# Pool's long element-wise operations in pieces, first norm's squares added on VectorE, second layer's first norm summed earlier, three Newton steps in place of four

## The chip, the cores and the metric

One core of one Trainium2 chip runs the whole program. The metric is the device time of one execution in microseconds (us). The time before is 2428.57 us, the median of 3 runs (2425.60 to 2429.08).

## The reference

A trunk of two layers on 16 learned meta tokens followed by 512 tokens, so T = 528, with rows of 1024 channels. Each layer is a norm, one input projection, two parallel branches, a gated merge, and an MLP. All weights and data are float32.

```
xn = rms_norm(h, norm1_g)                       # h * rsqrt(mean(h*h) + EPS) * g
z, xbc, dt_raw, q, k, v, gates = split(xn @ w_in)
y_ssd  = ssd_mixer(z, xbc, dt_raw, ...)         # conv, silu, chunked scan, 8 groups, group norm
y_attn = sliding_window_attention(q, k, v, ...) # rms_norm and rotary on q and k, window 128, sinks
merged = g_ssd * (y_ssd @ w_ssd_down) + g_attn * (y_attn @ w_attn_down)
h = h + merged @ w_o
h = h + square(relu(rms_norm(h, norm2_g) @ w_mlp_up)) @ w_mlp_down
```

The norms of q and k are over 64 channels of a head. The output is h without the meta tokens.

## The kernel before

Activations lie transposed: 128 channels on the partitions, tokens along the columns, so h is 8 rows of 128x528 (`h(k)`). Every dense product is made in a split of float32 into two rounded parts, `hi` and `lo = x - hi`: each weight tile (1024x128, `wraw`) is loaded by DMA, rounded by ScalarE into `whi`, and VectorE or GpSimd (Pool) subtracts to get `wlo`; TensorE then runs three passes of 8 matmuls (hi by hi, lo by hi, hi by lo) for each span of columns (266 or 264, or 512 in the parts that leave the meta tokens out). There are 172 weight tiles a layer, and two buffers each for `wraw`, `whi` and `wlo`.

The order on every engine is written by a planner in Python, the class `Flow`. It keeps a clock for each engine (`F.t`), costs each instruction by a formula, and pins the program order. Dense products run in a fixed order; the rest are generator tasks in queues (`w` for weights, `post`, `misc`, `tail`, `chunk`, `attn`), which `tick` steps forward between matmuls once the plan has their inputs ready. So a change of one cost moves instructions of all engines further on. `tt_any` (line 434 ff.) gives an element-wise operation to Pool (`G`) if the plan has it end there earlier than on VectorE (`V`) with a margin; the `wlo` subtractions, the rotary products and parts of attention and of the y rows go through it.

The places that the change touches:

- **Program start.** DMAs on SP's queue load `h` (8 rows), then the first constants (`cst`, whose `ones` column every sum needs), then the weights of v. For each row ScalarE squares it (`sq`), and TensorE adds over channels with five matmuls by `ones`, one for each chunk of tokens, into five banks; `rms_tok` turns the sums into the norm's factor `rt` (five small operations on VectorE, one power on Pool). `bcast_tok` spreads it over partitions (TensorE), VectorE multiplies `h` by it, ScalarE writes `hnh`, VectorE `hnl`, and the products with the weights of v (`wvh`, `wvl`, 288 columns: v and dt) begin.
- **Layer 1, first norm.** The products of v start from rows of h without the norm's factor (`hgh`, `hgl`; 8 rows, hi and lo in turn), since the factor of a token is applied afterwards. `norm` adds squares over channels, as `cst,acc` and `cst,sq` matmuls; a task that `tick` steps when its rows are planned to be ready. The normed rows (`hnh`, `hnl`) are made from its factor by `normal_row` and are needed by the first tile of k.
- **Norms of q and k.** `rsqrt` runs on VectorE: a start from integer arithmetic (`rqs`), then four Newton steps of three operations on 128x20 to 128x40 elements, then a copy. It is called once for k and twice for q in each layer, and the attention scores of the heads wait for it.
- **Pool's operations.** `wlo` is one operation of 128x1024, `q` (lo part of the queries) 64x512, the rotary product `qa`, `kn` 128x528 or 128x512, `t` the same, and in `tail` one of the two products by the gate 128x528 or 128x512.

Of the kernel before, what the change touches and what calls it, by code (L numbers as in the profile page):

```python
# [17 lines left out]
P = 128  # L18
# [28 lines left out]
CCOL = {}  # L47
# [307 lines left out]
def hybrid_trunk_kernel(ctx: ExitStack, tc: tile.TileContext, h0, params, consts, rope, wdt, w, out,  # L355
# [80 lines left out]
    def tt_any(out, a, b, op, spare=None):  # L436

        n = Engine.size(out)
        eng = G if max(F.t["g"], F.t["pe"]) + n * 2.09 + 125.0 < max(F.t["v"], F.t["pe"]) + n / 0.96 + (F.SPARE if spare is None else spare) else V
        eng.tensor_tensor(out=out, in0=a, in1=b, op=op)  # L440
# [151 lines left out]
    def rms_tok(sq, inv_n, cs, tag, rows=(), bank="ps", sums=None):  # L592


        if not sums:
            yield {bank: 1, "after": rows, "data": lambda: [x[:, CHUNKS[cs[0]][0]:sum(CHUNKS[cs[-1]])] for x in sq()]}
            ps = Slot("ps")
            for c in cs:
                t0 = CHUNKS[c][0]
                x = sq()  # L600
                for i in range(len(x)):
                    mm(ps.t[:, c:c + 1], x[i][:, t0:t0 + P], C("ones"), start=i == 0, stop=i == len(x) - 1)
# [3 lines left out]
        for c in cs if sums else (cs[0],):  # L606
            y, z = (x[:, c:c + 1], sums[c].t[:, 0:1]) if sums else (x, ps.t[:, c:cs[-1] + 1])
            V.tensor_scalar(out=y, in0=z, scalar1=inv_n, scalar2=EPS, op0=ALU.mult, op1=ALU.add)
        for z in sums or (ps,):
            z.free()  # L610
# [61 lines left out]
    F.dma(par[:, 0, 0:KD], params[:, 0, 0:KD])  # L672
    for k in range(KD):
        F.dma(h(k), h0[:, k, :])
    few = CCOL["low"][0]
    F.dma(cst[:, 0:few], consts[:, 0:few])
# [12 lines left out]
    sums = [Slot("ps") for _ in CHUNKS]  # L689
    for k in range(KD):  # L690
        sq = Slot(min(("zs", "sq", "xh", "raw"), key=lambda n: F.rings[n].at()), "sq")
        S.activation(out=sq.t, in_=h(k), func=AF.Square)
        for c in range(5):
            t0 = CHUNKS[c][0]
            mm(sums[c].t[:, 0:1], sq.t[:, t0:t0 + P], C("ones"), start=k == 0, stop=k == KD - 1)
        F.end = F.t["pe"]
        sq.free()
# [16 lines left out]
    for l in range(depth):  # L714
# [144 lines left out]
        for k in range(KD + 1):  # L859
            F.force(rows_[k:k + 1])  # L860
            if k < KD:
# [43 lines left out]
        def rope_tile(kind, spans, m, dst, c_lo):  # L905
# [15 lines left out]
            def rest():  # L921
# [8 lines left out]
                G.tensor_tensor(out=dst[:, lo:T], in0=qx[:, lo:T], in1=cosg[:, lo:T], op=ALU.mult)  # L930
# [19 lines left out]
        def rsqrt(x, t):  # L950
# [5 lines left out]
            for _ in range(4):  # L956
# [324 lines left out]
        def tail(gr, zs, cs):  # L1281
# [6 lines left out]
            for j in range(2):  # L1288
                (G if j else V).tensor_tensor(out=xs[j], in0=xs[j], in1=sq[j][:, a:b], op=ALU.mult)
# [456 lines left out]
```

## Time and profile before

| | |
|---|---|
| time, median of 3 runs | 2428.57 us |
| time of the profiled execution | 2423.47 us |
| span of the profiled execution | 2421.3 us |
| TensorE busy | 2361.0 us (98%) |
| VectorE (DVE) busy | 1313.1 us (54%) |
| ScalarE (ACT) busy | 1024.9 us (42%) |
| Pool busy | 1101.8 us (46%) |
| mean granted clock of TensorE | 0.995 |

A busy VectorE is counted from the start of an instruction to its end, with what it waits inside the instruction. Busy TensorE says nothing of its clock. Most instructions of VectorE, ScalarE and Pool are issued by one helper and stand under line L348, matmuls under L431 and transposes under L434, so they are told apart by their tiles.

### The profile page before, as it was taken

The page shows a single profiled execution, that of the slowest core. Times are in us where ns is not written, and L with a number is a line of the kernel's source. Part 1 is how long each engine was busy: PE and PEld are TensorE (multiplying, and loading weights), DVE is VectorE, ACT ScalarE, POOL GpSimd, SP SyncE. Part 2 cuts the span into 40 slices and gives each one's busy share as a digit, 9 for nine tenths or more (in the row PEclk, how much of TensorE's full clock was granted, in tenths as well). Part 3 has the DMA queues.
Part 4 walks back from the last instruction along what each step waited for, and adds up shares of the span by engine and source line. Part 5 has one row for each costly group of instructions (what it writes and reads, how often), then busy time and mean ns, then how long its engine had stood idle before and what let it go on. Part 6 is the DMA issues. An engine that isn't in the chain of part 4 may idle for free.

```text
span 2421.3 us, 40518 instructions
## 1 busy us (share of the span) xinstructions
PE 2361.0 (98%) x16098; PEld 2148.4 (89%) x16098; DVE 1313.1 (54%) x2505; ACT 1024.9 (42%) x1999; POOL 1101.8 (46%) x659
## 2 busy tenths in 40 slices
PE   7999999999999999999999899999999999999999
PEld 7998999999999999999998778888987788888887
DVE  3686879787423444233247868787874145433221
ACT  3455665654422233223244456656554223333231
POOL 2734444465444334434435444445555544444443
PEclk9999999999999999999999999999999999999999
DMA  3323333343453322222232233334434433222222
GB/s 122 105 79 98 93 103 93 102 115 102 121 180 111 134 85 88 89 96 88 99 133 86 66 104 106 110 80 115 112 105 127 176 120 135 96 95 93 94 93 104
DMA packets 133578, 257.33 MB, mean 106 GB/s; under 512 B 16470, under 2 KB 66318, under 8 KB 133390
## 3 DMA queue, kind: packets, MB, share of 16 engines
q1 hardware_dynamic: 133390, 254.75, 33.1%
q8 instruction: 127, 2.08, 0.3%
q14 instruction: 61, 0.50, 0.1%
HBM read 232.03 MB, written 17.33 MB: 103 GB/s over the span
## 4 chain that ended last, share of the span: by engine, by line
PE 82%; DVE 12%; issue 2%; DMA 1%; ACT 1%; POOL 1%; SPq 0%; DVEq 0%; POOLq 0%; ACTq 0%
PE ps L431 80%; PE ps L434 2%; DVE at L348 2%; DVE raw L348 2%; DVE xb L348 1%; DVE rqs L348 1%; DVE xh L348 1%; DVE ar L348 1%; DMA gm<-ac_dram 1%; DVE gm L348 1%; DVE qa L348 0%; DVE hnl L348 0%; DVE es L348 0%; DVE h L348 0%; DVE mx L348 0%
## 5 line engine op out<-in xcount | busy, mean ns | idle before, releaser
L348 POOL TENSOR_TENSOR wlo<-wraw,whi 128x1024 fp32r<-128x1024 f32 x326 | 793.4, 2434 | 950.0 <-ACT whi L348 880.5
L348 ACT CAST whi<-wraw 128x1024 fp32r<-128x1024 f32 x340 | 355.4, 1045 | 708.0 <-PE ps L431 412.9
L431 PE MATMUL ps<-hnh,whi 128*128 128x266 f32 (+2 forms) x2048 | 398.7, 311 | 5.6 <-ACT hnh L348 4.8
L431 PE MATMUL ps<-hnl,whi 128*128 128x266 f32 (+2 forms) x2048 | 395.7, 310 | 0.0
L431 PE MATMUL ps<-hnh,wlo 128*128 128x266 f32 (+2 forms) x2048 | 389.6, 308 | 0.0
L431 PEld LDWEIGHTS ps<-hnh,whi 128*128 128x128 f32 x2048 | 304.4, 190 | 21.4 <-ACT hnh L348 6.2
L431 PEld LDWEIGHTS ps<-hnl,whi 128*128 128x128 f32 x2048 | 304.2, 190 | 15.1 <-issue 1.8
L431 PEld LDWEIGHTS ps<-hnh,wlo 128*128 128x128 f32 x2048 | 302.7, 190 | 15.3 <-issue 2.7
L348 DVE SCALAR_TENSOR_TENSOR h<-ps,h 128x264 f32<-128x264 f32 (+1 forms) x120 | 62.1, 518 | 308.6 <-PE ps L431 308.6
L348 DVE TENSOR_TENSOR hidl<-s,hidh 128x528 fp32r<-128x528 f32 (+1 forms) x64 | 116.8, 1824 | 87.9 <-ACT s L348 87.9
L431 PE MATMUL ps<-hgl,whi 128*128 128x264 f32 (+1 forms) x768 | 153.7, 322 | 1.3 <-DVE hgl L348 1.3
L431 PE MATMUL ps<-hgh,wlo 128*128 128x264 f32 (+1 forms) x768 | 153.3, 321 | 0.0
L431 PE MATMUL ps<-hgh,whi 128*128 128x264 f32 (+1 forms) x768 | 152.8, 320 | 0.0
L431 PE MATMUL ps<-hidl,whi 128*128 128x264 f32 (+1 forms) x768 | 152.7, 320 | 0.0
L431 PE MATMUL ps<-hidh,whi 128*128 128x264 f32 (+1 forms) x768 | 152.5, 320 | 0.0
L431 PE MATMUL ps<-hidh,wlo 128*128 128x264 f32 (+1 forms) x768 | 152.5, 320 | 0.0
L431 PE MATMUL ps<-y,whi 128*128 128x264 f32 (+1 forms) x768 | 137.0, 320 | 0.0
L431 PEld LDWEIGHTS ps<-hgl,whi 128*128 128x128 f32 x768 | 119.1, 189 | 12.4 <-DVE hgl L348 1.6
L431 PEld LDWEIGHTS ps<-hgh,wlo 128*128 128x128 f32 x768 | 119.3, 189 | 11.1
L431 PEld LDWEIGHTS ps<-hidl,whi 128*128 128x128 f32 x768 | 118.8, 188 | 11.0
L431 PEld LDWEIGHTS ps<-hidh,wlo 128*128 128x128 f32 x768 | 118.7, 188 | 11.1
L431 PEld LDWEIGHTS ps<-hidh,whi 128*128 128x128 f32 x768 | 118.6, 188 | 11.1
(220 smaller groups left out, 3949.5 us busy)
## 6 DMA issues: line engine op xcount, KB each, us to landing
wraw<-w_dram SPq DMA_DIRECT2D x344, 512.0 KB
gm<-ac_dram SPq DMA_DIRECT2D x64, 256.0 KB
et<-ac_dram SPq DMA_DIRECT2D x128, 64.0 KB
t<-au SPq DMA_DIRECT2D x48, 66.0 KB
h<-h_dram SPq DMA_DIRECT2D x8, 264.0 KB
at<-rope_dram SPq DMA_DIRECT2D x4, 528.0 KB
y_dram<-xb SPq DMA_DIRECT2D x4, 528.0 KB
yr<-y_dram SPq DMA_DIRECT2D x8, 264.0 KB
```

Of the source, the lines that this page charges most:

```text
L348: inst = fn(*a, **k)
L431: F.run("pe", cost, [o], [lhsT, rhs], PE.matmul(out=o, lhsT=lhsT, rhs=rhs, start=start, stop=stop))
L434: F.run("pe", 108.0 if in_.shape[1] > 64 else 60.0, [o], [in_], PE.transpose(out=o, in_=in_, identity=C("ident", k)[:, :k]))
```

## The change

1. `tt_any` issues an operation that goes to Pool and has 512 columns or more in pieces of at most 256 (for a tile of several rows: row by row where a row is longer). The rotary product on Pool is cut in two at column 264, the gate's product in `tail` in two halves.
2. At the start, the first constants are loaded after the fifth row of h and no longer after the eighth. The squares of the 8 rows are added on VectorE into the first (7 additions of 128x528), and TensorE sums that one row over channels with 5 matmuls into one bank, where it had 40 into five. While rows arrive, TensorE multiplies each of the first seven by itself (128x264, float32) into a bank that nothing reads.
3. In layer 1, before the products of row 5 for v, all rows of h are forced into the order and the norm's sums are issued.
4. `rsqrt` makes three Newton steps.

```
         eng = G if ... else V
-        eng.tensor_tensor(out=out, in0=a, in1=b, op=op)
+        if eng is V or n < 512:
+            eng.tensor_tensor(out=out, in0=a, in1=b, op=op)
+            return
+
+        if len(out.shape) == 2:
+            m = -(-n // 256)
+            at = [n * i // m for i in range(m + 1)]
+            for x, y in zip(at, at[1:]):
+                eng.tensor_tensor(out=out[:, x:y], in0=a[:, x:y], in1=b[:, x:y], op=op)
+            return
+        m = out.shape[1]
+        step = max(1, m * 256 // n)
+        for x in range(0, m, step):
+            y = min(x + step, m)
+            eng.tensor_tensor(out=out[:, x:y], in0=a[:, x:y], in1=b[:, x:y], op=op)
...
+    few = CCOL["low"][0]
     for k in range(KD):
         F.dma(h(k), h0[:, k, :])
-    few = CCOL["low"][0]
-    F.dma(cst[:, 0:few], consts[:, 0:few])
+        if k == 4:
+            F.dma(cst[:, 0:few], consts[:, 0:few])
...
-    sums = [Slot("ps") for _ in CHUNKS]
+    busy = Slot("ps")
+    kinds = ("zs", "sq", "xh", "raw")
+    total = None
     for k in range(KD):
-        sq = Slot(min(("zs", "sq", "xh", "raw"), key=lambda n: F.rings[n].at()), "sq")
+        sq = Slot(min(kinds, key=lambda n: F.rings[n].at()), "sq")
         S.activation(out=sq.t, in_=h(k), func=AF.Square)
-        for c in range(5):
-            t0 = CHUNKS[c][0]
-            mm(sums[c].t[:, 0:1], sq.t[:, t0:t0 + P], C("ones"), start=k == 0, stop=k == KD - 1)
-        F.end = F.t["pe"]
-        sq.free()
+        if k < KD - 1:
+            mm(busy.t[:, 0:T // 2], h(k)[:, 0:P], h(k)[:, 0:T // 2])
+        if total is None:
+            total = sq
+        else:
+            V.tensor_tensor(out=total.t, in0=total.t, in1=sq.t, op=ALU.add)
+            F.end = F.t["v"]
+            sq.free()
+    busy.free()
+    sums = Slot("ps")
+    for c in range(5):
+        t0 = CHUNKS[c][0]
+        mm(sums.t[:, c:c + 1], total.t[:, t0:t0 + P], C("ones"))
...
         for k in range(KD + 1):
             F.force(rows_[k:k + 1])
+            if l and k == KD - 3:
+
+                F.force(rows_)
+                while norm_t[0].needs.get("after") is not None:
+                    F.step(norm_t[0], F.queues["misc"])
...
-                G.tensor_tensor(out=dst[:, lo:T], in0=qx[:, lo:T], in1=cosg[:, lo:T], op=ALU.mult)
+                for x, y in ((lo, 264), (264, T)):
+                    G.tensor_tensor(out=dst[:, x:y], in0=qx[:, x:y], in1=cosg[:, x:y], op=ALU.mult)
...
-            for _ in range(4):
+            for _ in range(3):
...
-            for j in range(2):
-                (G if j else V).tensor_tensor(out=xs[j], in0=xs[j], in1=sq[j][:, a:b], op=ALU.mult)
+            V.tensor_tensor(out=xs[0], in0=xs[0], in1=sq[0][:, a:b], op=ALU.mult)
+            h_ = (b - a) // 2
+            for x, y in ((0, h_), (h_, b - a)):
+                G.tensor_tensor(out=xs[1][:, x:y], in0=xs[1][:, x:y], in1=sq[1][:, a + x:a + y], op=ALU.mult)
```

How the instructions move, at three places. A row is line, operation, output and inputs, size, and how often it stands in a row.

**TensorE at the program's start**, before:

```order
L431 MATMUL ps<-cst,sq 128x1 x40
L431 MATMUL ps<-cst,rt 128x16
L431 MATMUL ps<-cst,rt 128x128 x4
L431 MATMUL ps<-wvh,hnh_192 128x288 x10
L431 MATMUL ps<-wvl,hnh_192 128x288 x4
```

and after:

```order
L431 MATMUL ps<-h_80 128x264 x4
L431 MATMUL ps<-h_81 128x264 x3
L431 MATMUL ps<-cst,sq 128x1 x5
L431 MATMUL ps<-cst,rt 128x16
L431 MATMUL ps<-cst,rt 128x128 x4
L431 MATMUL ps<-wvh,hnh_164 128x288 x10
```

The 40 sums become 5, behind the seven products of h by itself; on VectorE the seven additions stand ahead of a single `rt<-ps 128x5`. VectorE also gets a subtraction `wvl<-wraw,wvh 128x7x128` and a `wvl<-rawdt,wvh 128x7x32` behind its first `hnl`, where it had 128x128 and 128x32; Pool has the smaller ones now.

**VectorE at layer 1's first norm**, from the factor `rt` to the first `dtx` (which waits for the last products of v), before:

```order
L348 TENSOR_SCALAR rt<-ps 128x5
L348 TENSOR_SCALAR na<-na 128x32
L348 TENSOR_TENSOR h_9718<-h_9718,ps 128x272
L348 TENSOR_TENSOR h_9718<-h_9718,ps 128x256
L348 SCALAR_TENSOR_TENSOR hnl_14216<-h_9718,par,hnh_14214 128x528
L348 SCALAR_TENSOR_TENSOR dtx<-ps,rt,par 128x32
```

and after (the products `h<-h,ps` of six rows of h stand there, of which these are the last two, where before there were four rows):

```order
L348 TENSOR_TENSOR h_10012<-h_10012,ps 128x272
L348 TENSOR_TENSOR h_10012<-h_10012,ps 128x256
L348 SCALAR_TENSOR_TENSOR hnl_14725<-h_10011,par,hnh_14723 128x528
L348 TENSOR_TENSOR h_10012<-h_10012,ps 128x272
L348 TENSOR_TENSOR h_10012<-h_10012,ps 128x256
L348 SCALAR_TENSOR_TENSOR hnl_14726<-h_10012,par,hnh_14724 128x528
L348 SCALAR_TENSOR_TENSOR dtx<-ps,rt,par 128x32
```

On TensorE the ten sums `cst,acc` and `cst,sq` stand behind 45 products of v, where they stood behind 68.

**Pool in layer 1 beside the norms of the first four tiles of q**, before:

```order
L348 TENSOR_TENSOR wlo<-wraw,whi 128x1024
L348 TENSOR_TENSOR q_14980<-qa_14591,q_14980 64x512
L348 TENSOR_TENSOR q_14986<-qa_14591,q_14986 64x512
L348 TENSOR_TENSOR qa_14592<-au,at 128x512
L348 TENSOR_TENSOR wlo<-wraw,whi 128x1024
L348 TENSOR_TENSOR qa_14592<-au,at 128x512
L348 TENSOR_TENSOR t_15015<-t_15015,at 128x512
```

and after:

```order
L348 TENSOR_TENSOR wlo<-wraw,whi 128x256 x4
L348 TENSOR_TENSOR q_15506<-qa_15102,q_15506 64x256 x2
L348 TENSOR_TENSOR q_15513<-qa_15102,q_15513 64x256 x2
L348 TENSOR_TENSOR qa_15103<-au,at 128x248
L348 TENSOR_TENSOR qa_15103<-au,at 128x264
L348 TENSOR_TENSOR wlo<-wraw,whi 128x256 x4
L348 TENSOR_TENSOR t_15479<-t_15479,at 128x256 x2
```

The same work in the same order, each operation cut in two or four. Over the whole program 326 operations `wlo` of 128x1024 on Pool become 1264 of 128x256 (316 weight tiles; VectorE makes 24 in place of 14).

## Rows read from the trace of the kernel before

**Rows 1.** The page's first part: busy us, share, instructions; and the clock by core.

```profile
PE 2361.0 (98%) x16098; PEld 2148.4 (89%) x16098; DVE 1313.1 (54%) x2505; ACT 1024.9 (42%) x1999; POOL 1101.8 (46%) x659
...
core 0: 2421.3 us, clock 0.995
```

**Rows 2.** Busy by stretch: us; PE, PEld, DVE, ACT, POOL; PEclk; DMA share, GB/s.

```profile
34.00:600.00 566.00, 552.87 (x4438) 523.25 (x4439) 441.37 (x1026) 321.43 (x775) 282.99 (x201) 1.00 0.34 98
600.00:1246.00 646.00, 643.15 (x5271) 639.80 (x5270) 230.69 (x328) 200.48 (x292) 270.01 (x130) 1.00 0.32 111
1246.00:1860.00 614.00, 588.31 (x3883) 513.36 (x3882) 470.60 (x982) 330.02 (x717) 300.06 (x216) 0.99 0.36 101
```

**Rows 3.** Waits of TensorE's matmuls from 34 us on: us in total, times, longest us.

```profile
PE ps L431 <- DVE ar L348: 13.3, 16, 2.2
...
PE ps L431 <- DVE rqk L348: 3.7, 1, 3.7
PE ps L431 <- POOL xdd L348: 2.2, 2, 1.7
```

**Rows 4.** Timeline of TensorE at the start: start us, us, work [idle before <-releaser].

```profile
11.39 17.20 PE L431 MATMUL ps<-cst,sq 128*128 128x1 f32 x80 [11.39 <-DMA cst<-consts_dram]
30.10 2.61 PE L431 MATMUL ps<-cst,rt 16*128 16x16 f32 x10 [1.51 <-POOL rt L348]
33.99 2.77 PE L431 MATMUL ps<-wvh,hnh 128*128 128x288 f32 x10 [1.28 <-ACT hnh L348]
```

**Rows 5.** Timeline of ACT at the start.

```profile
8.29 1.30 ACT L348 ACTIVATE sq<-h 128x528 f32<-128x528 f32 x2 [1.41 <-DMA h<-h_dram]
...
18.55 2.16 ACT L348 CAST wvh<-wraw 128x896 fp32r<-128x896 f32 x4
```

**Rows 6.** Timeline of DVE before layer 1: an addition like the new ones.

```profile
1232.28 0.70 DVE L348 TENSOR_TENSOR acc<-acc,sq 128x528 f32<-128x528 f32 x1
```

**Rows 7.** Timeline of PE and DVE at layer 1's first norm.

```profile
1254.63 0.28 PE L431 MATMUL ps<-cst,acc 128*128 128x1 f32 x2
...
1259.88 1.68 DVE L348 TENSOR_TENSOR h<-h,ps 128x272 f32<-128x272 f32 x4 [2.67 <-PE ps L431]
...
1260.52 5.46 PE L431 MATMUL ps<-wvl,hgh 128*128 128x288 f32 x40
...
1273.17 0.81 PE L431 MATMUL ps<-hnh,whi 128*128 128x264 f32 x2 [4.76 <-ACT hnh L348]
```

**Rows 8.** Timeline of Pool, DVE and PE at the norms of layer 1's first q tiles.

```profile
1335.70 2.34 POOL L348 TENSOR_TENSOR wlo<-wraw,whi 128x1024 fp32r<-128x1024 f32 x1
...
1329.24 2.41 DVE L348 TENSOR_SCALAR rqs<-rqk 128x32 int32<-128x32 int32 x1
...
1335.82 2.27 DVE L348 TENSOR_TENSOR rqs<-rqk,rqs 128x32 f32<-128x32 f32 x1
...
1341.24 0.19 DVE L348 TENSOR_TENSOR rqs<-rqk,rqs 128x32 f32<-128x32 f32 x1
...
1341.92 0.18 DVE L348 COPY rqk<-rqs 128x32 f32<-128x32 f32 x1
...
1342.74 1.87 PE L431 MATMUL ps<-cst,au 128*128 128x2 f32 x8 [6.63 <-DVE mx L348]
```

**Rows 9.** Busy by stretch, the stretch behind that wait of TensorE.

```profile
1341.20:1348.00 6.80, 5.26 (x16) 4.52 (x17) 5.58 (x28) 2.73 (x14) 0.00 (x0) 0.50 0.01 2
```

**Rows 10.** Groups by form on Pool: busy us, mean ns | idle before, releasers.

```profile
L348 POOL TENSOR_TENSOR wlo<-wraw,whi 128x1024 fp32r<-128x1024 f32 x326 | 793.4, 2434 | 950.0 <-ACT whi L348 880.5 <-DMA wraw<-w_dram 42.6 <-PE ps L431 11.1
...
L348 POOL TENSOR_TENSOR xdd<-xdt,ddt 128x256 f32<-128x256 f32 x48 | 32.9, 685 | 70.6 <-DVE xdt L348 60.0 <-PE ps L431 5.7 <-DVE cb L348 4.7
...
L348 POOL TENSOR_TENSOR qa<-au,at 128x512 f32<-128x512 f32 x8 | 10.3, 1282 | 0.2
```

**Rows 11.** Timeline of Pool in the MLP of layer 1.

```profile
2074.40 2.40 POOL L348 TENSOR_TENSOR wlo<-wraw,whi 128x1024 fp32r<-128x1024 f32 x1 [4.05 <-ACT whi L348]
2079.94 2.41 POOL L348 TENSOR_TENSOR wlo<-wraw,whi 128x1024 fp32r<-128x1024 f32 x1 [3.14 <-ACT whi L348]
```

More of the change, by code (lines that the diff above doesn't have):

```diff
@@ L592, in rms_tok @@
     def rms_tok(sq, inv_n, cs, tag, rows=(), bank="ps", sums=None):
+        ps = sums
         if not sums:
@@ L605, in rms_tok @@
         x = r[:, cs[0]:cs[-1] + 1]
[L606 to L610, printed above, removed]
+        V.tensor_scalar(out=x, in0=ps.t[:, cs[0]:cs[-1] + 1], scalar1=inv_n, scalar2=EPS, op0=ALU.mult, op1=ALU.add)
+        ps.free()
         G.tensor_tensor(out=x, in0=x, in1=C("mhalf")[:, cs[0]:cs[-1] + 1], op=ALU.pow)
@@ L687, in hybrid_trunk_kernel @@
     hs_dram = dr.tile([P, KD, T], F32, name="hs_dram")
-    sums = [Slot("ps") for _ in CHUNKS]
+    busy = Slot("ps")
+    kinds = ("zs", "sq", "xh", "raw")
+    total = None
     for k in range(KD):
-        sq = Slot(min(("zs", "sq", "xh", "raw"), key=lambda n: F.rings[n].at()), "sq")
+        sq = Slot(min(kinds, key=lambda n: F.rings[n].at()), "sq")
         S.activation(out=sq.t, in_=h(k), func=AF.Square)
-        for c in range(5):
-            t0 = CHUNKS[c][0]
-            mm(sums[c].t[:, 0:1], sq.t[:, t0:t0 + P], C("ones"), start=k == 0, stop=k == KD - 1)
-        F.end = F.t["pe"]
-        sq.free()
+        if k < KD - 1:
[11 more added lines that the diff above has]
+        mm(sums.t[:, c:c + 1], total.t[:, t0:t0 + P], C("ones"))
+    F.end = F.t["pe"]
+    total.free()
     def first_norm():
```

## The prediction

> **What bounds the kernel now.** I read the busy times first: TensorE works 2361.0 of 2421.3 us [rows 1], so the whole program can gain at most its 60.3 us of idle time, and what a low clock costs it. The mean granted clock is 0.995 [rows 1]; time missing at half rate is 0.005 x 2421.3, some 12 us. Everything else VectorE, ScalarE, Pool and the DMAs do lies under TensorE's work, so a term below counts only where TensorE stands still or runs slow.
>
> Next, where it stands still. The table by stretch shows 13.1 us in 34 to 600 (layer 0's mixers), 2.9 in 600 to 1246 (merge and MLP: nothing to be had), 25.7 in 1246 to 1860 (layer 1's mixers) [rows 2]. The start has 11.39 + 1.51 + 1.28 = 14.2 us, and there even the busy time is poor: 17.20 us go into the forty small sums [rows 4]. Then the waits: behind the start TensorE waits almost only for VectorE, in short waits (16 for `ar`, 13.3 us), but for one of 3.7 us for `rqk` and one of 6.63 us in layer 1 [rows 3, 8], and once for ScalarE's `hnh`, 4.76 us [rows 7].
>
> Last, why VectorE is late. Its operation on 128x32 elements takes 0.19 us alone (1341.24), but 2.41 and 2.27 us at 1329.24 and 1335.82 [rows 8]; the second starts 0.12 us behind a `wlo` of Pool and ends at 1338.09, which is 0.05 us behind that `wlo`'s end at 1338.04. So VectorE's operations that read two tensors, or copy, stand until Pool's operation is over, and get one turn between two of Pool's.
>
> **The start: -13.5 us.** Now: the constants land at 11.39, sums until 28.59, TensorE's first product for v at 33.99 [rows 4]. After: the constants are the sixth transfer, so the last of the same nine, now h's eighth row, should land near 11.4, where the last one landed before. Its square takes 0.65 (1.30 for two) [rows 5], the addition 0.70 [rows 6]: 12.8 with a hand-over of 0.1. The other six additions fit between the rows' landings. Five sums are ten records at 17.20/80 = 0.215 us: 2.15 us, ending near 15.0. The way from the last sum to the first v product stays what it is, 33.99 - 28.59 = 5.4: 20.4. Gain 33.99 - 20.4 = 13.6. VectorE gets a larger share of `wvl` behind row 0, roughly 0.7 us more on a stretch that it sets; Pool's pieces give about that back to its `hnl`. I take 13.5. If the clock were up by then, the ten records, ten of `rt` and so on would save some 2 us more: 15.5. From the other side, v's weights are rounded at 18.55 to 21.1 now, behind the last square [rows 5]; were that their landing and not the queue, v's products could not start before 21.9 (one more row of `hnh`), a gain of 12; with the 0.7 us and a late `wvl`, 10.5. The seven products of h by itself cost nothing: TensorE has no other work until the sums.
>
> Here the Trainium skill speaks ("TensorE: Matmul & The Clock Gate", Part 1): the half rate is the default, and sustained activity releases it. By that the seven products would raise the clock before the sums, and the term would be -15.5. The row speaks less plainly: TensorE ran 17.2 us without a pause on 128x1 sums and still needed 0.215 us for each [rows 4], so activity of some kind was not enough. My sum takes no gain from it.
>
> **Layer 1's first norm: -2.7 us.** The sums stand behind 45 products in place of 68; 23 at 5.46/40 = 0.136 us are 3.1 us, less what the first ones overlap, so they begin at about 1251.9 and not at 1254.63 [rows 7]. VectorE can begin its rows 2.7 us before 1259.88, which makes two more rows (1.36 us each) ahead of its work for v's results, as the new order has it. TensorE's wait of 4.76 us [rows 7] loses that much. Bounds: 0 (the squares of the last row come late, and TensorE waits for them inside the v products) and -3.1.
>
> **Norms of q: -4.5 us.** From 1329.24 to 1342.10 VectorE makes 15 operations; Pool meanwhile makes seven, and the last two Newton steps run free, 0.68 us each (1341.24 to 1341.92) [rows 8]. After: 12 operations, each behind at most one piece. A piece's price is not in the trace; nearest rows are 0.685 us for 128x256 with a broadcast operand, and the line through 2434 ns for 1024 and 1282 for 512 columns, 0.13 + 0.576 = 0.71 [rows 10]. I take 0.71, since it is the same operation. 12 turns of 0.71 + 0.05 are 9.1 us: VectorE ends at 1338.4, 3.7 us earlier, if Pool is never idle. TensorE's 6.63 us of idle time shrinks by that much. At the 3.7 us wait of layer 0, Pool's backlog ends earlier anyway, so I count the dropped step there and a little more, 0.8. Bounds: -1.4 (two dropped steps) and -10.3 (both waits gone).
>
> **The other waits for VectorE: -9 us.** Idle time behind 34 us less the three waits named is 46 - 15 = 31 us, of it 4.4 behind 1860. An operation that meets a whole `wlo` waits 1.2 us on average, with a piece 0.36. That would take two thirds; but Pool needs longer in total and takes a turn between any two operations of VectorE, so I take a third, -9. Bounds: 0 and -20.
>
> **The clock: -3.5 us.** Behind the 6.63 us wait TensorE is granted 0.50, that is 1.2 GHz, for 6.8 us [rows 9]: 3.4 us lost. I count one such stretch as gone, of the 12 us. Bounds: 0 and -9.
>
> **Pool's longer work: 0.** Four pieces cost 4 x 0.71 = 2.84 us for 2.43, 0.4 us more, by 316 tiles 128 us: Pool 1230 of 2400 us. It hides under 950 us in which Pool waits before `wlo`, most of it for `whi` [rows 10]; in the MLP a tile lasts 5.54 us and `wlo` 2.4 of them [rows 11]. Against cutting speaks what the skill says of Pool ("GPSIMD Engine Reference", 2.1): each instruction is dispatched by software, for tens of cycles. As an estimate, that is under 0.1 us for each piece, where the rows' line has 0.13; with either the sum stays the same.
>
> **Sum.** 13.5 + 2.7 + 4.5 + 9 + 3.5 = 33.2. Against the profiled execution: 2423.5 - 33.2 = 2390.3. That execution is 5.1 us below the median of the runs, so the median to expect is 2428.6 - 33.2 = **2395 us**.
>
> **Rivals.**
>
> *The pieces give nothing* (0.20). Pool's turns come one for one, so what VectorE saves in one operation it loses over four; the planner's new order makes as many new waits as it ends. For it: the chain at 1329 had to wait for seven operations of Pool, and with 12 pieces it waits as often as it asks. Against: 0.71 is less than a third of 2.4. Then start, norm and two dropped steps are left: 13.5 + 2.7 + 1.4 = 17.6, 2411 us.
>
> *The pieces free nearly all waits* (0.11). Upper bounds of the last terms: 13.5 + 2.7 + 10.3 + 20 + 6 = 52.5, 2376 us.
>
> *Pool becomes late* (0.05), the slower side. Place: the groups of the scan (34 to 600, 1246 to 1860), where VectorE is busy 75 to 78% [rows 2] and can hold each piece of Pool for one of its operations (0.7 us). A `wlo` then lasts up to 2.84 + 3 x 0.7 = 4.9 us, and `xdd`, `st` and `xb` of the scan stand behind it. TensorE waits 2.2 us for `xdd` now [rows 3]. There are 80 chunks in the two layers; 0.6 us for each would be 48 us: 2428.6 + 48 - 17.6 = 2459 us. It decides once Pool is busy over some four fifths of those stretches; it is at one half now (283 of 566), and at 56% with 0.4 us for each tile. The point where it eats up all gains is 0.2 us a chunk above the other new waits.
>
> *The start's gain is eaten by a new order* (0.04). From the first change on, every instruction is planned anew; a few waits like the one of 6.63 us in new places make 2424 to 2433 us.
>
> **Numbers.** Forecast 0.60, rivals 0.20, 0.11, 0.05, 0.04. The likeliest case alone: 2384 to 2405. The range of 8 in 10 takes in the second case and most of the third: 2379 to 2417. A measurement of this kernel can tell about 0.2% (5 us) from no change. Faster: the first three cases, 0.91; within 0.2%: 0.04; slower: 0.05.
>
> **What would show it.** Right: TensorE's first v product at 20 to 21 us; ten sums of layer 1 some 2.7 us earlier in their stretch; VectorE's small operations below 0.9 us beside Pool; Pool busy near 1230 us with pieces near 0.71; fewer waits for `ar`; fewer stretches at 0.50. Wrong: waits of TensorE for `xdd`, `st` or `wlo`; a Pool far above 1300 us; waits as long as before in other places, by which the second case would hold.

## The result, and the profile after

The changed kernel takes 2388.27 us (median of 4 runs, 2387.16 to 2394.63) against 2428.75 us before: a ratio of 0.984, 95% interval 0.983 to 0.985, or 40.5 us less. The forecast was 2395 us with a range of 2379 to 2417. The profiled execution took 2389.05 us with a span of 2387.3 us. Between the two profiled executions the difference is 34.4 us, since that of before lay 5.3 us below its median and that of the changed kernel 0.8 us above.

The page's first part and the clock by core, changed kernel; [rows 1] has the same of before:

```profile
PE 2350.3 (98%) x16042; PEld 2142.1 (90%) x16042; DVE 1170.8 (49%) x2501; ACT 1024.7 (43%) x1999; POOL 1306.5 (55%) x1711
...
core 0: 2387.3 us, clock 0.990
```

TensorE is idle for 37.0 us in place of 60.3. VectorE is busy 142 us less although it has no less to do (seven more additions and ten more `wlo`, against 18 Newton operations and four of `rt` less). Some 120 of the 142 us, by an estimate that counts what each instruction takes over the shortest of its form, are time spent standing inside an instruction. Pool is busy 205 us more. The mean clock is lower, not higher; in part that is because the record of the clock begins at 37.3 us in the kernel before and at 10.0 here.

To see where the time went I cut both executions at the same products: TensorE's first product for v, the first product of the merge (`ah`), the same two in layer 1, and the end.

| stretch | before: us | after: us | difference |
|---|---|---|---|
| start to the first v product | 34.0 | 19.3 | -14.7 |
| layer 0's mixers | 643.1 | 643.5 | +0.4 |
| merge and MLP of layer 0 | 569.2 | 567.4 | -1.8 |
| layer 1's mixers | 634.9 | 615.8 | -19.2 |
| merge and MLP of layer 1, and the end | 540.1 | 541.3 | +1.2 |

The two stretches of mixers by the table of busy times (us; PE, PEld, DVE, ACT, POOL; PEclk; DMA share, GB/s), before and then after:

```profile
33.99:677.09 643.10, 629.97 (x5072) 597.71 (x5072) 475.86 (x1095) 355.82 (x850) 319.45 (x229) 1.00 0.35 101
1246.29:1881.24 634.95, 609.26 (x3973) 530.37 (x3972) 471.79 (x986) 335.57 (x725) 310.71 (x222) 0.99 0.35 102
```

```profile
19.32:662.82 643.50, 633.63 (x5071) 603.46 (x5072) 459.29 (x1095) 356.24 (x850) 356.19 (x470) 0.98 0.35 100
1230.21:1845.97 615.76, 604.48 (x3973) 530.02 (x3972) 436.18 (x982) 336.88 (x727) 342.48 (x452) 0.99 0.36 105
```

Stretch less PE's busy time is TensorE's idle time: in layer 0 it falls from 13.1 to 9.9 us, but the busy time grows by 3.7, at a clock of 0.98. In layer 1 the idle time falls from 25.7 to 11.3 us and the busy time by 4.8.

TensorE's waits after (us in total, times, longest), against [rows 3]:

```profile
PE ps L431 <- DVE ar L348: 4.5, 5, 2.8
PE ps L431 <- POOL xdd L348: 3.2, 3, 1.7
PE ps L431 <- POOL q L348: 2.7, 2, 1.9
PE ps L431 <- DVE mx L348: 1.9, 2, 1.1
...
PE ps L431 <- POOL rx L348: 1.4, 1, 1.4
PE ps L431 <- DVE vm L348: 1.3, 1, 1.3
```

Five waits for `ar` are left of sixteen, and the waits of 6.6 us for `mx` and 3.7 for `rqk` are gone. New or longer ones are at most 2.8 us: one for `ar`, and most of the others name Pool (`q`, `rx`, `xdd`).

The start, by TensorE's timeline after ([rows 4]):

```profile
12.44 1.47 PE L431 MATMUL ps<-cst,sq 128*128 128x1 f32 x10 [1.55 <-DVE sq L348]
15.43 2.61 PE L431 MATMUL ps<-cst,rt 16*128 16x16 f32 x10 [1.52 <-POOL rt L348]
19.32 2.77 PE L431 MATMUL ps<-wvh,hnh 128*128 128x288 f32 x10 [1.28 <-ACT hnh L348]
```

The norms of layer 1's first q tiles, by the timelines of Pool, VectorE and TensorE after ([rows 8]):

```profile
1316.87 2.84 POOL L348 TENSOR_TENSOR wlo<-wraw,whi 128x256 fp32r<-128x256 f32 x4 [2.06 <-ACT whi L348]
1319.78 3.00 POOL L348 TENSOR_TENSOR q<-qa,q 64x256 fp32r<-64x256 f32 x4
...
1316.69 0.18 DVE L348 TENSOR_SCALAR rqs<-rqk 128x32 int32<-128x32 int32 x1
1316.90 0.75 DVE L348 TENSOR_SCALAR rqs<-rqs 128x32 int32<-128x32 int32 x1
1317.68 0.68 DVE L348 TENSOR_TENSOR rqs<-rqk,rqs 128x32 f32<-128x32 f32 x1
1318.39 1.37 DVE L348 SCALAR_TENSOR_TENSOR rqs<-rqs 128x32 f32<-128x32 f32 x2
...
1323.67 0.66 DVE L348 COPY rqk<-rqs 128x32 f32<-128x32 f32 x1
...
1324.96 1.05 PE L431 MATMUL ps<-cst,au 128*128 128x2 f32 x8 [1.13 <-DVE mx L348]
```

An operation of VectorE that takes 0.19 us alone now takes about 0.7 beside a piece, where it took up to 2.41 beside a whole operation. The chain of 12 lasts from 1316.69 to 1324.33, 7.6 us; the 15 of before lasted 12.9. The wait for `mx` behind it is 1.13 us in place of 6.63.

### The profile page after: what moved, and what is told of

Same layout as the page of the kernel before. It is cut to its first block, busy times and chain, and to the rows that moved or that the text cites. A ratio compares the mean times of both kernels' runs of the same rounds, so it can differ in the third digit from the quotient of the medians.

```text
span 2387.3 us, 41696 instructions
## 1 busy us (share of the span) xinstructions
PE 2350.3 (98%) x16042; PEld 2142.1 (90%) x16042; DVE 1170.8 (49%) x2501; ACT 1024.7 (43%) x1999; POOL 1306.5 (55%) x1711
## 4 chain that ended last, share of the span: by engine, by line
PE 90%; DVE 5%; DMA 1%; POOL 1%; ACT 1%; issue 1%; SPq 0%; DVEq 0%; POOLq 0%; ACTq 0%
PE ps L431 87%; PE ps L434 2%; DVE at L348 1%; DMA gm<-ac_dram 1%; DVE raw L348 1%; POOL wlo L348 0%; DVE xb L348 0%; DVE rqs L348 0%; DVE xh L348 0%; DVE h L348 0%; DVE hnl L348 0%; DVE ar L348 0%; ACT whi L348 0%; ACT gm L348 0%; DMA cst<-consts_dram 0%
## 5 line engine op out<-in xcount | busy, mean ns | idle before, releaser
L348 POOL TENSOR_TENSOR wlo<-wraw,whi 128x256 fp32r<-128x256 f32 x1264 | 979.9, 806 | 803.5 <-ACT whi L348 790.3
L431 PE MATMUL ps<-hnh,wlo 128*128 128x266 f32 (+2 forms) x2048 | 398.7, 310 | 0.0
L431 PE MATMUL ps<-hnh,whi 128*128 128x266 f32 (+2 forms) x2048 | 392.1, 309 | 5.3 <-ACT hnh L348 3.9
L348 DVE SCALAR_TENSOR_TENSOR tmp<-ps,rbc 128x264 f32<-128x264 f32 (+1 forms) x96 | 49.5, 515 | 179.0 <-PE ps L431 170.2
L431 PEld LDWEIGHTS ps<-hgl,whi 128*128 128x128 f32 x768 | 119.3, 189 | 11.5 <-DVE hgl L348 0.6
L431 PEld LDWEIGHTS ps<-hgh,whi 128*128 128x128 f32 x768 | 119.3, 189 | 11.1
L431 PEld LDWEIGHTS ps<-hidh,wlo 128*128 128x128 f32 x768 | 118.8, 188 | 11.1
```

The source lines that it names most:

```text
L348: inst = fn(*a, **k)
L431: F.run("pe", cost, [o], [lhsT, rhs], PE.matmul(out=o, lhsT=lhsT, rhs=rhs, start=start, stop=stop))
```

## The experiments

Stretches in the table are cut as above; "idle" is TensorE's idle time in them, read from its timeline. Differences are to the kernel before in the same comparison; ratios with their 95% interval.

| kernel | us | difference | ratio | layer 0: us (idle) | layer 1: us (idle) |
|---|---|---|---|---|---|
| before | 2428.75 | | | 643.1 (13.1) | 634.9 (25.7) |
| changed | 2388.27 | -40.5 | 0.9839 (0.9826 to 0.9851) | 643.5 (9.9) | 615.8 (11.3) |
| start alone | 2415.98 | -10.1 | 0.9959 (0.9946 to 0.9971) | 646.1 (14.0) | 638.0 (25.7) |
| pieces alone | 2409.97 | -16.1 | 0.9934 (0.9921 to 0.9946) | 647.3 (12.0) | 622.4 (14.7) |
| early sums alone | 2434.86 | +8.8 | 1.0039 (1.0025 to 1.0052) | 645.6 (12.9) | 640.6 (29.4) |
| three steps alone | 2439.89 | +13.8 | 1.0055 (1.0042 to 1.0069) | 655.0 (22.3) | 634.1 (24.2) |
| changed, whole operations | 2432.55 | +4.4 | 1.0021 (1.0011 to 1.0031) | 658.1 (23.5) | 641.8 (29.2) |
| changed, no products of h | 2389.27 | -38.9 | 0.9831 (0.9814 to 0.9848) | 646.4 (11.6) | 615.3 (10.9) |
| changed, four steps | 2386.03 | -42.2 | 0.9828 (0.9815 to 0.9842) | 636.8 (6.6) | 622.7 (14.0) |
| changed, late sums | 2394.95 | -33.3 | 0.9856 (0.9842 to 0.9871) | 647.7 (10.4) | 618.4 (11.5) |
| old order, pieces | 2409.81 | -16.5 | 0.9933 (0.9919 to 0.9946) | 643.5 (12.1) | 620.6 (14.9) |
| new order, whole | 2414.68 | -11.6 | 0.9949 (0.9936 to 0.9961) | 647.8 (14.9) | 631.6 (24.5) |
| new order, 512 columns | 2404.97 | -24.3 | 0.9899 (0.9884 to 0.9914) | 648.8 (13.4) | 631.1 (21.9) |
| new order, 128 columns | 2408.58 | -17.7 | 0.9921 (0.9908 to 0.9935) | 656.5 (19.8) | 627.5 (16.8) |

### The parts one by one

**Start alone.** The edit is part 2 of the change and nothing else (the constants as the sixth transfer, the additions on VectorE, the products of h by itself, one bank of sums).

> Before with the start of the change alone: squares added on VectorE, the seven products of h by itself, constants as the sixth transfer. Theory A (a saving of its own place): TensorE's first v product at 19 to 20 us in place of 33.99, and the rest of the program as before: 2428.7 - 14.7 = 2414 us, give or take 3. Theory B (the clock gives it back): with the earlier start the half-rate stretches that the changed kernel shows at 54, 95 and 112 to 122 us (8.5 us lost against 1.7 in the kernel before) come with this part alone, so some 7 us are given back in layer 0: 2421 us.

Measured: 2416.0 us, 10.1 less, between the two theories. The first v product is at 18.73 us, 15.3 us earlier than before, but only two thirds of it reach the end. Timeline of TensorE, start alone:

```profile
18.73 2.77 PE L431 MATMUL ps<-wvh,hnh 128*128 128x288 f32 x10 [1.28 <-ACT hnh L348]
...
33.26 0.94 PE L431 MATMUL ps<-wvh,hnl 128*128 128x288 f32 x5 [1.86 <-DVE hnl L348]
34.04 6.98 PE L431 MATMUL ps<-wvl,hnh 128*128 128x288 f32 x40
```

VectorE, beside whole operations of Pool, is 1.86 us late with the last row, and the forty `wvl` products that follow take 6.98 us where layer 1's took 5.46 [rows 7]; the granted clock is 0.50 from 34.50 to 37.91 us. The first product for k comes at 40.85 us against 53.70 before, so 12.9 us of the 15.3 are left there. In the changed kernel it comes at 38.28, 15.4 us earlier: the pieces keep VectorE in time. Theory A's number for the start is right, and what it left out is that the start needs the pieces. Another 3.0 us are lost in layer 1's mixers, at the same idle time: TensorE stands there at half rate for 24 us, where it did for 17. That is theory B's cause, though not in the places that theory B named.

**Pieces alone.** Part 1 of the change and nothing else.

> Before with Pool's long operations in pieces alone. Theory A (pieces end the waits for VectorE): the changed kernel's layer 1 from its first v product to the merge is 19.2 us shorter, and this comes from the pieces: 2428.7 - 17 to 20 = 2409 to 2412 us, TensorE's waits for ar under 7 us of 13.3, Pool's pieces 0.80 us on average. Theory B (turns one for one, and a new order): the pieces alone give under 5 us, 2424 to 2429 us, and layer 1's gain comes from the other parts or from how they fall together.

Measured: 2410.0 us, as theory A has it; the waits for `ar` fall to 4.7 us. The largest part is layer 1's idle time, 25.7 to 14.7 us; layer 0 is 4.2 us longer in the profiled execution, at half rate for 25 us where it was for 7.

**Early sums alone.**

```diff
+            if l and k == KD - 3:
+                F.force(rows_)
+                while norm_t[0].needs.get("after") is not None:
+                    F.step(norm_t[0], F.queues["misc"])
```

> Before with layer 1's first sums moved ahead alone. Theory A (the prediction's term): the sums 2.4 us earlier in their stretch, TensorE's wait for hnh of 4.76 us 2.7 shorter: 2426 us. Theory B (what the changed kernel's trace hints: there the k products end 0.9 us later behind the first v product, not earlier): nothing, 2427 to 2430 us, the time that VectorE wins is spent ahead of the same row.

Measured: 8.8 us slower, which neither theory had. Up to layer 1's sums TensorE's order is that of the kernel before, so only layer 1 can answer for the edit: its mixers are 5.7 us longer, with 3.7 us more idle time. The rest of the 8.8 us lies where the two kernels have the same instructions; this difference alone says nothing of the sums. Over the whole execution the idle time grows by 2.5 us and TensorE's busy time by 6.9, so most of the loss is time at a low clock: at the same mean clock, 0.991, a run of before took 2432.0 us and one of this kernel 2432.7.

**Three steps alone.**

```diff
-            for _ in range(4):
+            for _ in range(3):
```

> Before with three Newton steps in place of four alone (one step less of the reciprocal root; the result moves in its last digits). Theory A (the step's own time in the two places where TensorE waits for it, 0.7 us each when free, up to 3 x 2.4 us beside whole operations of Pool): 2422 to 2427 us, the wait of 6.63 us in layer 1 shorter. Theory B (Pool sets the pace there, not the number of operations): 2428 to 2430 us, the wait as long as before.

Measured: 13.8 us slower; both theories' times fail. The wait in layer 1 is shorter, 4.37 us for 6.63, and that for `rqk` in layer 0 is gone, as theory A wanted; but at the same place in layer 0 stands a longer one, of 5.96 us for `mx`. Waits of TensorE, three steps alone ([rows 3] for before):

```profile
PE ps L431 <- DVE ar L348: 14.4, 13, 2.2
PE ps L431 <- DVE mx L348: 10.3, 2, 6.0
...
PE ps L431 <- POOL xdd L348: 6.7, 5, 2.9
```

Three operations of 0.19 us less let the planner put attention and scan in another order from there on, and layer 0's idle time goes from 13.1 to 22.3 us. Over the whole execution idle time grows by 6.6 us and TensorE's busy time by 5.5.

### The parts taken out of the changed kernel

**Whole operations.** The three places of part 1 undone; the planner makes its order anew.

> The changed kernel with Pool's operations whole again; start, early sums and three steps stay. Theory A (parts add): the pieces gave 16 us alone, so 2388 + 16 = 2404 us, between 2400 and 2410. Theory B (the pieces carry the other parts: with whole operations every shift in the order brings new waits, as the early sums alone cost 8.7 us and the dropped step alone 13.8): the three other parts by their runs alone give 2426.1 - 10.1 + 8.7 + 13.8 = 2438; anything from 2418 upward speaks for it.

Measured: 2432.6 us, slower than the kernel before, by theory B. The pieces, worth 16 us alone, are worth 45 with the other parts (from 4.4 more than before to 40.5 less). Layer 0 has 23.5 us of idle time and layer 1 29.2.

**No products of h by itself.**

```diff
-        if k < KD - 1:
-            mm(busy.t[:, 0:T // 2], h(k)[:, 0:P], h(k)[:, 0:T // 2])
```

> The changed kernel without the seven products of h by itself. Their product is read by nobody, so nothing of the result is left out. Theory A (they raise the clock for the ten sums and no further): sums at 0.215 us each as in the kernel before, 0.7 us more, first v product at 20 to 20.4, the total 2388.5 to 2391 us. Theory B (they decide the clock in layer 0's first products too): half rate to beyond 24 us and more such stretches before 130 us, 2393 us and more.

Measured: 2389.3 us, theory A. The five sums (ten records) take 2.29 us in place of 1.47 and the first v product is at 19.88 in place of 19.32; at the first `wvl` product, 33.57 against 33.02, the difference is still 0.55 us, and in the total it is lost in the scatter. The products raise the clock for the sums, and these runs show nothing more of them.

**Four steps.** The loop of `rsqrt` back to `range(4)`.

> The changed kernel with four Newton steps. Theory A (the step costs its three operations at two places on TensorE's path, 0.7 us each behind a piece): 2390 to 2393 us. Theory B (the order decides; the step alone made the kernel before 13.8 us slower): the time moves by over 4 us either way, with waits in other places, and the two places where TensorE waits for the norms of q stay as long as they are.

Measured: 2386.0 us, not told apart from the changed kernel, and so neither theory's total. At the two places the step has its price, as theory A has it: TensorE waits 3.17 us for `mx` in place of 1.13, and 3.04 for `rqk` in layer 0 where the changed kernel waits 2.7 for `q`. But layer 0 is 6.7 us shorter and layer 1 is 6.9 longer: the order moves time about as theory B has it, and the two cancel. A fourth step costs nothing here that can be measured.

**Late sums.** The added lines of part 3 removed.

> The changed kernel with layer 1's first sums back at the end of the 68 products. Theory A (the prediction's term): VectorE begins its rows 2.4 us later, the two waits for hnh and vm of 5.2 us grow by that: 2391 us. Theory B (the sums' place is worth nothing, since VectorE spends the time won on other operations ahead of the same row): 2386 to 2389 us; if the run alone (8.7 us slower with them early) holds here too, 2380 us.

Measured: 2395.0 us, above both theories' numbers. VectorE begins its rows 1.6 us later, as theory A has it, but layer 1's idle time is 11.5 us against 11.3, so the waits that theory A names did not grow. Layer 0, whose instructions are in the same order in both, is 4.2 us longer in this execution, its idle time 0.5 us. What is left is TensorE's busy time at a low clock (see the end): the granted clock is 0.50 for 12 us more of this execution than of the changed kernel's, 6.1 us of work, and the two executions differ by 6.3. Runs of the two kernels at the same mean clock are 1 to 2 us apart (2394.6 against 2395.4 and 2396.6 at 0.988, 2387.2 against 2389.5 at 0.992). So the sums' place is worth 2 us at the most, near theory B. Whether it also brings the low clock, or chance does, stays open.

### Order and length held apart

Each run so far mixes two things, since every edit makes the planner arrange all later instructions anew. In the next four the order of every engine is held, instruction by instruction, and only the form in which Pool's operations are issued differs:

```diff
+        for s in issue:
+            F.pin("g", nc.gpsimd.tensor_tensor(out=out[:, s], in0=a[:, s], in1=b[:, s], op=op))
+        for s in plan:
+            o = out[:, s]
+            F.run("g", Engine.size(o) * 2.09 + 125.0, [o], [a[:, s], b[:, s]], None)
```

`plan` is what the planner counts (whole, or pieces of 256), `issue` is what Pool gets; `run` with None pins no instruction.

**Old order, pieces.**

> Every engine's order of the kernel before, kept instruction by instruction; only Pool's long operations are issued in pieces (the planner still counts each as whole). Theory A (the pieces as such shorten VectorE's waits, in any order): near the 2410 us that the pieces gave with a new order, 2405 to 2415. Theory B (the gain is in the order that the planner finds for pieces): 2422 to 2430 us.

Measured: 2409.8 us. The pieces as such give 16.5 us in the very order that was made for whole operations; theory A. Waits of TensorE, old order with pieces; they were 13.3 us for `ar` [rows 3] and 6.63 for `mx` [rows 8]:

```profile
PE ps L432 <- DVE ar L349: 5.1, 10, 0.9
...
PE ps L432 <- DVE mx L349: 3.2, 1, 3.2
```

**New order, whole.**

> Every engine's order of the changed kernel, kept instruction by instruction, start, early sums and three steps included; only Pool's long operations are issued whole, where the first piece stood. Theory A (pieces as such): 2420 to 2435 us, TensorE's waits for ar, mx and q back to 20 us and more. Theory B (the order): 2388 to 2400 us.

Measured: 2414.7 us, a little below theory A's span and far above theory B's. Waits of TensorE, new order with whole operations:

```profile
PE ps L432 <- DVE ar L349: 17.4, 12, 2.9
...
PE ps L432 <- DVE mx L349: 6.6, 1, 6.6
...
PE ps L432 <- POOL q L454: 2.8, 2, 2.4
```

`ar`, `mx` and `q` together are 26.8 us against 9.1 in the changed kernel. The pieces are worth 28.9 us in this order (11.6 to 40.5), and what remains of the change without them, 11.6 us, is less than the 14.7 us at the start. The order that the planner makes for whole operations (4.4 us more than before) is 16 us worse still.

At a held order the gain is idle time of TensorE, not clock. From the first v product to the last product it goes from 42.4 to 28.8 us in the old order and from 43.0 to 22.9 in the new one, while the time at half rate stays nearly the same (27 and 29 us in the old order, 37 and 38 in the new; up to 37 us of the old order it is read from the pace of the products, since the record of the clock begins there).

**128 columns.**

> The changed kernel's order, Pool's pieces half as long (128 columns). By the line 0.13 us + 0.56 us for 256 columns a piece costs 0.42 us alone: a wlo 3.3 us, Pool near 1450 us busy. Theory A (what VectorE waits for one piece decides): some 2 to 6 us less, 2382 to 2386 us. Theory B (the turns one for one decide: Pool loses a turn of VectorE between any two pieces): Pool over 1500 us, TensorE waits for Pool's xdd, q and rx over 10 us in place of 8, 2392 us and more.

Measured: 2408.6 us, theory B in every number: Pool is busy 1539.8 us, and TensorE now waits for Pool (15.4 us for `xdd`, `rx` and `q`, 7.3 in the changed kernel). Pool's groups by form and TensorE's waits, 128 columns:

```profile
L454 POOL TENSOR_TENSOR wlo<-wraw,whi 128x128 fp32r<-128x128 f32 x2528 | 1183.1, 503 | 634.3 <-ACT whi L349 614.6 <-DVE mx L349 12.5 <-DMA wraw<-w_dram 3.2
```

```profile
PE ps L432 <- POOL xdd L349: 9.3, 9, 2.8
...
PE ps L432 <- DVE rqs L349: 4.6, 1, 4.6
...
PE ps L432 <- POOL rx L349: 4.3, 3, 3.3
```

**512 columns.**

> The changed kernel's order, Pool's wlo in two pieces of 512 columns in place of four of 256 (the products with cosine and the tails' halves whole). So far at this order: whole 2414.7 us, 256 columns 2388.3, 128 columns 2408.6. Theory A (two prices against each other: VectorE's wait for a piece grows with its length, 1.28 us for 512; Pool's loss of a turn and 0.13 us grow with their number): between, 2392 to 2404 us, Pool near 1180 us, TensorE's waits for ar above 7 us. Theory B (one turn of VectorE in a wlo is enough): 2380 to 2388 us, a version that beats both.

Measured: 2405.0 us, 1 us above theory A's span; theory B is out. The waits for `ar` are 11.1 us, and the one of 6.6 us for `mx` is as long as with whole operations.

So at one order the gain against before goes 11.6 us (1024 columns), 24.3 (512), 40.5 (256), 17.7 (128). On VectorE's side the cause is seen in one row, the Newton operations by tile (shortest, median and longest in ns behind the count): before, new order with 512, changed, 128 columns.

```profile
L348 DVE SCALAR_TENSOR_TENSOR rqs<-rqs x48: 178/194/2433, 81.7 to 1378.4; 128x20 f32<-128x20 f32 x16, 128x40 f32<-128x40 f32 x16, 128x32 f32<-128x32 f32 x16
```

```profile
L349 DVE SCALAR_TENSOR_TENSOR rqs<-rqs x36: 178/196/1328, 61.9 to 1374.2; 128x20 f32<-128x20 f32 x12, 128x40 f32<-128x40 f32 x12, 128x32 f32<-128x32 f32 x12
```

```profile
L348 DVE SCALAR_TENSOR_TENSOR rqs<-rqs x36: 178/196/790, 62.3 to 1357.5; 128x20 f32<-128x20 f32 x12, 128x40 f32<-128x40 f32 x12, 128x32 f32<-128x32 f32 x12
```

```profile
L349 DVE SCALAR_TENSOR_TENSOR rqs<-rqs x36: 178/199/493, 61.9 to 1374.9; 128x20 f32<-128x20 f32 x12, 128x40 f32<-128x40 f32 x12, 128x32 f32<-128x32 f32 x12
```

The longest is one operation of Pool each time: 2433, 1328, 790, 493 ns, where a `wlo` operation of Pool beside which VectorE runs nothing takes 2399, 1289, 736 and 459 ns. The Trainium skill ("SBUF — State Buffer", "SBUF: two separate sides") says that a Pool operation that reads SBUF and a VectorE operation with two inputs in SBUF contend for a shared pair of ports, an exclusive lock that the first holds for its whole instruction while the other stands; these four rows, of an operation with two such inputs, agree. On Pool's side the price is in its group: a piece of 128 columns takes 503 ns on average, so a `wlo` 4.0 us, against 806 and 3.2 with 256 columns (next section).

No version here beats the changed kernel by more than can be measured.

## Why the prediction was right, and where not

The time (2388 against 2395) and the mechanism that carries it (VectorE's operations stand for one operation of Pool, so shorter ones end waits) are right; of the single terms three were off.

How near the sum came is in part luck. Cut at the same products, the start gave 14.7 us (forecast 13.5), idle time behind it 18.4 (forecast 16.2 for three terms), and TensorE's busy time behind it 1.0 (forecast 3.5 for the clock): 34.1 us in all against 33.2, with errors that cancel. Of the 7 us between the two medians, 2395 and 2388, most is that the profiled execution of before was a fast one, 5.3 us below its median, and that of the changed kernel was not.

**The start, -13.5.** Right: -14.7 at the first v product (19.32; forecast 20.4), -15.4 at the first product for k. The result lies between the sum and its bound of 15.5 with the clock up: the added row was ready at 12.44 in place of 12.8, and the five sums (ten records) took 1.47 us, not 2.15; but the clock fell again at 13.37, and the ten records of `rt` took 2.61 us as before. The Trainium skill's rule cited there ("TensorE: Matmul & The Clock Gate", Part 1) holds for the seven products, by the runs with and without them. The worry about VectorE's `hnl` was right too, but only with whole operations of Pool, in the start alone (1.86 us).

**Layer 1's first norm, -2.7.** Wrong; it is about 0. The step that failed is "VectorE can begin its rows 2.7 us before", and with it that TensorE's wait loses as much. The rows of Pool, VectorE and TensorE in the changed kernel, from the timelines; behind them TensorE's first wait at this place in the kernel before ([rows 7] has its second):

```profile
1236.18 0.28 PE L431 MATMUL ps<-cst,acc 128*128 128x1 f32 x2
...
1238.33 1.22 PE L431 MATMUL ps<-wvh,hgh 128*128 128x288 f32 x5
...
1238.80 1.17 POOL L348 TENSOR_TENSOR rt<-rt,cst 128x5 f32<-128x5 f32 x1
...
1242.43 1.03 PE L431 MATMUL ps<-cst,rt 16*128 16x16 f32 x6
...
1243.49 1.68 DVE L348 TENSOR_TENSOR h<-h,ps 128x272 f32<-128x272 f32 x4 [4.83 <-PE ps L431]
...
1252.93 0.60 PE L431 MATMUL ps<-hnh,whi 128*128 128x264 f32 x3 [1.33 <-DVE vm L348]
...
1259.60 0.81 PE L431 MATMUL ps<-hnh,whi 128*128 128x264 f32 x2 [3.88 <-ACT hnh L348]
```

```profile
1266.60 0.60 PE L431 MATMUL ps<-hnh,whi 128*128 128x264 f32 x3 [0.49 <-DVE vm L348]
```

The sums do begin 2.4 us earlier, counted from the first v product (6.0 us behind it, 8.3 before): by the trace of before they stood behind 63 products and not 68, so 18 products were won and not 23. The factor is ready at 1239.97, but TensorE spreads it at 1242.43 only. In its order the spreading stands behind 18 more products for v (14 before), and 3.4 us of these ran at half rate (next part). So VectorE's rows begin 13.3 us behind the first v product, against 13.6 before.

That is not all. With four steps the same instructions stand here, and the clock behind the sums was full in that execution:

```profile
1233.10 1.68 DVE L348 TENSOR_TENSOR h<-h,ps 128x272 f32<-128x272 f32 x4 [3.30 <-PE ps L431]
...
1249.18 0.51 PE L431 MATMUL ps<-hnh,whi 128*128 128x264 f32 x2 [3.84 <-ACT hnh L348]
```

VectorE begins 11.8 us behind the first v product there, 1.8 us earlier than before, and still TensorE's two waits are 1.33 and 3.84 us, 5.2 together, against 0.49 and 4.76, 5.25, before. The two rows that were put ahead of VectorE's work for v's results push that work back, and behind it the last two rows: the wait did not go, it moved.

**Norms of q, -4.5.** The mechanism is right and the size near: 7.6 us for the chain (forecast 9.1), 5.5 us off the wait for `mx`. By the runs apart, pieces in the old order take 3.4 us off it (6.63 to 3.23), and the dropped step some 2.0 (3.17 with four steps, 1.13 with three, each in its own order). The wait for `rqk` in layer 0 is gone, and two for Pool's `q`, 2.7 us, stand near its place. The prediction says of the operations that stand that they read two tensors, or copy; its row at 1329.24 reads one and is no copy, and it took 2.41 us. That I priced the dropped step apart from the order was wrong: alone it costs 13.8 us, and in the changed kernel it brings nothing to the total.

**The other waits for VectorE, -9.** Right, and a little small: from the first v product to the last product TensorE's idle time falls by 19.5 us (42.4 to 22.9). Taken with the two terms before, the forecast was 16.2.

**The clock, -3.5.** Wrong in sign in layer 0. The stretches at half rate behind the 6.63 us wait and at 1764 us are gone. But new ones stand at 54, 95, 1239 and 1276 us, and the one near 120 us lasts from 112.4 to 122.6, where it was from 122.6 to 126.0 (end of this text). Layer 0's busy time grew by 3.7 us with them, layer 1's fell by 4.8. From the first v product to the last product half rate takes 38 us in place of 27, and the busy time falls by 1.0 us, where 3.5 was forecast.

**Pool's longer work, 0.** Right in effect, wrong in size: 1306.5 us busy, not 1230, with 806 ns for a piece and not 710. Group of Pool by form, changed kernel ([rows 10]):

```profile
L348 POOL TENSOR_TENSOR wlo<-wraw,whi 128x256 fp32r<-128x256 f32 x1264 | 979.9, 806 | 803.5 <-ACT whi L348 790.3 <-DVE mx L348 10.4 <-POOL q L348 1.4
```

At 1316.87 four pieces take 2.84 us, 0.71 each, as the line through the longer ones gave. Over the whole execution the 517 pieces beside which VectorE ran nothing took 736 ns each, the other 747 took 854 on average: the line was 26 ns short, and the rest of the 96 ns is what Pool stands for VectorE's operations, once a piece and not once a `wlo`. It still hides under 790 us of waiting for `whi`.

**The rivals.** "The pieces give nothing" is out by the two runs at a held order (16.5 and 28.9 us). "Pool becomes late" is a true mechanism at the wrong length: with 256 columns Pool is busy 55 to 56% of the two stretches of mixers, as forecast, and TensorE waits 3.2 us for `xdd`; with 128 it is busy 63 to 64% of them and the wait is 9.3. It decides from well below the four fifths that I named. "A new order eats the gain" is shown for whole operations: early sums alone, three steps alone, and all but the pieces together each made the kernel slower, although each takes work away or moves it forward. With the early sums alone most of that is low clock and not waits.

**What the sum hid.** I added the parts as if each had a price. They have none by themselves: alone they give -10.1, -16.1, +8.8 and +13.8, together -3.6, and the change gives -40.5. The kernel before stood in an order that suited whole operations; among whole operations an instruction of VectorE that is shifted to a bad place can cost up to 2.4 us, among pieces of 256 columns 0.8. The clock is part of it: from the first v product to the last product half rate takes 27 us in the kernel before and 29 in its order with pieces, but 36 to 57 in every execution with another order. In layer 1 every kernel with whole operations has 24 to 29 us of idle time, every one with pieces of 256 has 11 to 15. That the old order was the exception is my reading of these rows; no run tried many orders.

## What to carry to other kernels

Where two engines block each other for whole instructions, price a long operation by what the other engine's small ones wait for it, try its length at a held order, and expect an optimum: of the four lengths tried here, half the best lost 23 us of the gain and twice the best 16. In a kernel whose order a planner makes, an edit alone measures the edit and a new order together; hold the order and change one thing, or change the order and nothing else. Read idle time and granted clock apart when you compare two kernels. When you move a step forward, look whether the wait goes or only moves to what you put behind it.

## What the runs showed of the hardware

**The clock falls without an idle gap.** Busy times by stretch, changed kernel (PEclk behind the busy times):

```profile
47.50:54.30 6.80, 6.80 (x58) 6.27 (x58) 2.08 (x3) 2.77 (x9) 4.67 (x6) 1.00 0.36 112
54.30:57.70 3.40, 3.40 (x18) 3.40 (x17) 0.71 (x1) 0.60 (x2) 3.40 (x5) 0.50 0.46 139
...
1238.80:1242.20 3.40, 3.40 (x16) 3.40 (x15) 0.00 (x0) 2.36 (x5) 1.16 (x2) 0.50 0.48 160
```

From 47.5 to 54.3 us TensorE had no idle time by the profile (which models the ends of matmuls), and yet the granted clock was 0.50 behind it, 1.2 GHz. About half of what it did there were small products, 30 of the 58 records and 3.2 of the 6.8 us: the running sums of `adt` and the 2-column sums of squares for k (`cst,au`). Ahead of the stretch at 1238.8 stood the 1-column sums of layer 1's norm, again without a gap. At the start the products of h by itself follow each other every 0.44 us, and every 0.22 from 9.96 us on, where the clock is granted in full; it fell to half at 13.37, at the last of the ten records of 1-column sums and 2.5 us behind the last product of h. In the kernel before 17.2 us of 1-column sums alone ran at 0.213 us each from start to start, against 0.112 here ahead of the fall, so they did not raise the clock. At each of these places small products stood ahead of the low clock, and at the first two a TensorE without idle time did not prevent it. But they do not bring it by themselves: in the kernel before the same sums of layer 1 stand between the same products, from 1254.63 us on, and the clock stays full behind them:

```profile
1256.80:1260.20 3.40, 3.40 (x28) 3.21 (x27) 0.57 (x3) 0.00 (x0) 1.17 (x1) 1.00 0.00 0
```

Of the eight profiled executions with early sums six have a stretch at half rate behind them, of the six with late sums two. What decides stays open. The Trainium skill's rule ("TensorE: Matmul & The Clock Gate", Part 1), that sustained activity releases the half rate, does not tell these stretches from others by TensorE's busy time.

**The same order, another clock.** Up to layer 1's sums the changed kernel and the one with late sums have the same order on TensorE. Their profiled executions spend 643.5 and 647.7 us in layer 0's mixers, with 9.9 and 10.4 us of idle time, and at half rate they are for 21.4 us in the one (among others at 54 us, and from 112.4 to 122.6) and for 29.8 in the other (among others from 109.9 to 123.5, at 270 and at 571 us). Some 4 us of difference between two kernels can be this alone.
